# Where the weights begin in their tiles: the halves that stay in the array against those that move

## The chip, the cores and the metric

The kernel runs on one core of one Trainium2 chip. The metric is the time of one execution on the device in microseconds; the median of several runs counts.

## The reference

A decoder trunk of two layers over 256 tokens of width 1,024 in float32. The first layer is differential attention, the second attends with its own queries to a shared K and V (with 256 tokens there is one block of keys, so no others are selected). Each is followed by a squared-ReLU MLP with 4,096 hidden units, and both blocks end in a layer norm.

```python
for layer in range(DEPTH):
    if layer < N_A_LAYERS:
        mix = diff_attention(h, w_in_a[layer], lam_a[layer], subln_a[layer], w_out_a[layer], ...)
    else:
        if kv is None:
            kv = shared_kv(h, w_kv_shared)
        mix = moba_attention(h, w_q_b[j], w_out_b[j], kv[0], kv[1], kv[2], rel_bias)
    h = layer_norm(DEEPNORM_ALPHA * h + mix, ln1_g[layer], ln1_b[layer])
    h = layer_norm(DEEPNORM_ALPHA * h + squared_relu_mlp(h, w_up[layer], w_down[layer]), ...)
```

## The kernel before, in words

All weight matrices are cut into units of 128 x 2,048 numbers, 48 for each layer, in the order in which the program uses them. A unit comes in two pieces of 512 KB into the tiles `raw` (five buffers). ScalarE rounds a piece to a shorter format in `whi` (line 103), VectorE takes the difference, the remainder, to `wlo` (line 115). `whi` and `wlo` have seven buffers each (`AHEAD`), so unit v lies in slot v mod 7, and unit v + 7 waits until v has been used. The activations are split in the same way, into `act_hi` and `act_lo`, in the MLP into `h_hi` and `h_lo`. A product is then three matmuls: high by high, high by low, low by high; `three` issues them. It has two forms:

- *Weights move* (`moving_w`, lines 141 to 143): the activations of 128 tokens are loaded into the array as the stationary operand, and 512 columns of weights stream past. So it is for V, for the attention's output (`mix`), for the first quarter of the MLP's upward product (`up_rows`), and for the downward one (`down`). The end of the last layer's `down` streams 256 columns at a time.
- *Weights stay* (lines 145 to 147): 128 x 128 weights are loaded into the array, and the 256 tokens of `act` stream past. So it is for the queries and keys (`project`, units 2 to 9 in layer 0 and 4 to 11 in layer 1) and for the rest of the upward product (`up`, units 20, 21, 24, 25, and so on to 41 of each layer).

In a call of `nc.tensor.matmul` the output stands first, then the stationary operand, then the moving one; in the profile's rows the moving operand's tile stands first behind the arrow and the stationary one second. While one matmul streams, the weights of the next are loaded (the engine PEld of the profile).

Order: the program is written out by hand, engine by engine. Each `bg` call on the way does some pieces of later units, on ScalarE and VectorE, and starts their transfers on SyncE's queue.

Addresses: pools lie one behind the other in each partition. `act_hi` starts at byte 16,512, `act_lo` at 24,704, the seven `whi` at 70,336 and every 8,192 bytes behind it, the seven `wlo` at 127,680 in the same way. A tile `pad` of 96 bytes (line 64) stands ahead of the pools of the layers, so that `h_hi` and `h_lo` start at 202,368 and 214,656 and every 4,096 behind. Taken within 256 bytes that is 128 for the activations and 192 for the weights. All cuts into these tiles are by multiples of 512 bytes, so each matmul's operand keeps its tile's place within 512 bytes.

Of the kernel before, what the change touches and what calls it, by code (L numbers as in the profile page):

```python
# [21 lines left out]
F32R = mybir.dt.float32r  # L22
# [6 lines left out]
P = 128  # L29
# [13 lines left out]
UNITS = 48  # L43
AHEAD = 7
# [8 lines left out]
def trunk(ctx: ExitStack, tc: tile.TileContext, x, first, units, lam_a, subln, rel_bias,  # L53
# [4 lines left out]
    wpool = ctx.enter_context(tc.tile_pool(name="wpool", bufs=1))  # L58
# [2 lines left out]
    dram = ctx.enter_context(tc.tile_pool(name="dram", bufs=1, space=bass.MemoryType.DRAM))  # L61


    small.tile([P, 24], F32, name="pad", bufs=1)

    def bank(tag):
        return psum.tile([P, 512], F32, name="ps_" + tag, tag=tag,
                         bufs={"a": 4, "b": 2, "c": 2}[tag])

    def split_to(hi, lo, src, scale=None):  # L70

        nc.scalar.activation(hi, src, AF.Copy, scale=1.0 if scale is None else scale)  # L72
        if scale is None:
            nc.vector.tensor_tensor(lo, src, hi.bitcast(F32), op=ALU.subtract)  # L74
        else:
            nc.vector.scalar_tensor_tensor(lo, src, scale, hi.bitcast(F32),
                                           op0=ALU.mult, op1=ALU.subtract)
# [4 lines left out]
    raws, split, used, free = {}, {}, set(), set()  # L82
    state = {"piece": 0, "head": 0, "credit": 0.0}

    def fetch(q):

        if q < NU * PER:
            v, s = divmod(q, PER)
            raws[q] = wpool.tile([P, PIECE], F32, name="raw", bufs=RAWS)
            nc.sync.dma_start(raws[q], units[v, s])  # L90

    def head():

        v, s = divmod(state["head"], PER)
        if v >= NU:
            return False
        if s == 0 and v not in split:
            if v >= AHEAD and v - AHEAD not in free:
                return False
            split[v] = (wpool.tile([P, 2048], F32R, name="whi", bufs=AHEAD),  # L100
                        wpool.tile([P, 2048], F32R, name="wlo", bufs=AHEAD))
        c = slice(s * PIECE, (s + 1) * PIECE)
        nc.scalar.activation(split[v][0][:, c], raws[state["head"]], AF.Copy)  # L103
        state["head"] += 1
        return True

    def piece():

        while state["head"] < state["piece"] + 1 + LEAD and head():
            pass  # L110
        v, s = divmod(state["piece"], PER)
        if state["piece"] == state["head"]:
            return False
        c = slice(s * PIECE, (s + 1) * PIECE)
        nc.vector.tensor_tensor(split[v][1][:, c], raws.pop(state["piece"]), split[v][0][:, c].bitcast(F32),  # L115
                                op=ALU.subtract)
        fetch(state["piece"] + RAWS)
        state["piece"] += 1
        return True
# [35 lines left out]
    def at(k, h):  # L155
        return act[0][:, k, tokens(h)], act[1][:, k, tokens(h)]
# [181 lines left out]
    def attention(layer, u0):  # L338
# [4 lines left out]
        with tc.tile_pool(name=f"attn{layer}", bufs=2) as pool, \  # L343
# [19 lines left out]
            def v_first(u):  # L363

                if u == 0:
                    for h in range(2):
                        pv[0, h] = bank("a")
                split[u] = (wpool.tile([P, 2048], F32R, name="whi", bufs=AHEAD),
                            wpool.tile([P, 2048], F32R, name="wlo", bufs=AHEAD))
                hi, lo = (w.rearrange("p (k c) -> p k c", k=4) for w in split[u])  # L370
                for k in range(4):
                    kk = 4 * u + k
                    split_to(act[0][:, kk], act[1][:, kk], chunks[kk][:, :S])
                    split_to(hi[:, k], lo[:, k], chunks[kk][:, S:])
                    if 2 <= kk < NK - 1:
                        fetch(kk + 2)
                    if kk == 6:
                        nc.scalar.dma_start(scr, line)
                    a = [at(kk, h) for h in range(2)]
                    for h in range(2):  # L380
                        nc.tensor.matmul(pv[0, h], a[h][0], hi[:, k], start=kk == 0, stop=False)  # L381
                    for h in range(2):
                        nc.tensor.matmul(pv[0, h], a[h][1], hi[:, k], start=False, stop=False)
                    for h in range(2):
                        nc.tensor.matmul(pv[0, h], a[h][0], lo[:, k], start=False, stop=kk == NK - 1)
                state["piece"] = state["head"] = (u + 1) * PER
                state["credit"] += PACE
                used.add(u)

            if layer == 0:  # L390
                fetch_chunk(7, V[:, 0, :S + 512])
                v_first(0)
                v_first(1)
                free.update(used)
                bg()
                for h in range(2):
                    v_out(0, h)
            else:
                for h in range(2):
                    for c in range(2):  # L400
                        pv[c, h] = bank("a")
                        for g in range(2):
                            u = u0 + 2 * c + g
                            hi, lo = unit(u, k=4)
                            for k in range(4):
                                three(pv[c, h], (hi[:, k], lo[:, k]), at(4 * g + k, h), True, 1 / 8,
                                      g == 0 and k == 0, g == 1 and k == 3)
                                if (h, c, g) == (0, 1, 1) and k % 2 == 0:
                                    ln_turn(1, k // 2)
                            if h == 1:  # L410
                                used.add(u)
                                bg(2, True)
                        v_out(c, h)
# [567 lines left out]
```

## Time and profile before

| what | value |
|---|---|
| median of 3 runs | 592.87 us (592.8 to 593.11) |
| the profiled execution, its own time | 593.63 us |
| its span | 591.6 us |
| TensorE busy | 580.2 us (98%) |
| weight loads busy | 515.6 us (87%) |
| VectorE busy | 378.5 us (64%) |
| ScalarE busy | 318.3 us (54%) |
| moved by DMA | 113.03 MB, 191 GB/s in the mean |

The span is the time from the first to the last instruction that the profiler saw on the core; around it lie 2.0 us. Busy time of TensorE counts a matmul from its start to its modelled end, and matmuls overlap in the array. So a row's duration says little of how close one follows the other; the starts in the timeline do.

### The profile page before, as it was taken

Reading aid. Unit: us, or ns where it says so; the run is one execution under the profiler, and the core shown is the slowest. Engines: PE = TensorE matmul, PEld = TensorE weight load, DVE = VectorE, ACT = ScalarE, POOL = GpSimd, SP = SyncE. Lnnn points to the kernel's source line nnn. Section 1 sums busy time; section 2 is a strip of 40 time slices with the busy share of each in tenths; the row PEclk is TensorE's granted clock in tenths of the full one; section 3 lists DMA queues with packets and bytes.
Section 4 is the critical chain, followed back from the end, with each engine's and each line's share of the span. In section 5 each row is a group of like instructions: output and inputs, shape, how many; then the busy total and the mean of one; then the engine's idle time right before and its main releaser. Section 6 shows DMA issues by size and latency. Waiting matters only on the chain.

```text
span 591.6 us, 9649 instructions
## 1 busy us (share of the span) xinstructions
PE 580.2 (98%) x3768; PEld 515.6 (87%) x3768; DVE 378.5 (64%) x692; ACT 318.3 (54%) x540; POOL 13.1 (2%) x45
## 2 busy tenths in 40 slices
PE   9999999999999999999999999999999999999993
PEld 7999978889899899898889999878899899899883
DVE  5798778976744644543978677697785544554236
ACT  6676787257654655552447555642785564554100
POOL 2000020000000000000000000000000000000000
PEclk9999999999999999999999999999999999999998
DMA  8996736447745836755259744151798556553002
GB/s 300 327 337 229 243 116 212 174 150 268 271 172 207 277 126 237 248 168 191 83 170 344 256 150 155 54 178 36 242 324 288 175 183 214 187 170 107 1 0 71
DMA packets 35548, 113.03 MB, mean 191 GB/s; under 512 B 3872, under 2 KB 8880, under 8 KB 35504
## 3 DMA queue, kind: packets, MB, share of 16 engines
q1 hardware_dynamic: 34144, 107.95, 53.8%
q0 software_dynamic: 1152, 4.19, 2.4%
q8 instruction: 29, 0.48, 0.3%
q10 hardware_dynamic: 208, 0.29, 0.1%
q14 instruction: 15, 0.12, 0.1%
HBM read 111.35 MB, written 1.07 MB: 190 GB/s over the span
## 4 chain that ended last, share of the span: by engine, by line
PE 97%; DMA 1%; DVE 1%; ACT 0%; SPq 0%; issue 0%; DVEq 0%
PE ps_a L143 13%; PE ps_a L142 13%; PE ps_b L145 13%; PE ps_a L141 13%; PE ps_b L147 12%; PE ps_b L146 12%; PE ps_b L141 4%; PE ps_b L143 4%; PE ps_b L142 4%; PE ps_a L462 2%; PE ps_c L515 1%; PE ps_c L292 1%; DMA raw<-in_first 1%; PE ps_a L550 1%; PE ps_c L776 1%; PE ps_a L381 1%
## 5 line engine op out<-in xcount | busy, mean ns | idle before, releaser
L115 DVE TENSOR_TENSOR wlo<-raw,whi 128x1024 fp32r<-128x1024 f32 x188 | 222.8, 1220 | 55.1 <-ACT whi L103 54.7
L103 ACT ACTIVATE whi<-raw 128x1024 fp32r<-128x1024 f32 x188 | 190.1, 1052 | 71.6 <-PE ps_a L143 52.5
L145 PE MATMUL ps_b<-act_hi,whi 128*128 128x256 f32 x640 | 179.8, 281 | 0.0
L146 PE MATMUL ps_b<-act_lo,whi 128*128 128x256 f32 x640 | 177.5, 277 | 0.0
L147 PE MATMUL ps_b<-act_hi,wlo 128*128 128x256 f32 x640 | 177.5, 277 | 0.0
L145 PEld LDWEIGHTS ps_b<-act_hi,whi 128*128 128x128 f32 x640 | 120.2, 188 | 1.5 <-issue 0.7
L146 PEld LDWEIGHTS ps_b<-act_lo,whi 128*128 128x128 f32 x640 | 120.7, 189 | 0.5
L147 PEld LDWEIGHTS ps_b<-act_hi,wlo 128*128 128x128 f32 x640 | 120.3, 188 | 0.0
L143 PE MATMUL ps_a<-whi,h_lo 128*128 128x512 f32 x248 | 97.7, 394 | 0.0
L142 PE MATMUL ps_a<-wlo,h_hi 128*128 128x512 f32 x248 | 97.2, 392 | 0.0
L141 PE MATMUL ps_a<-whi,h_hi 128*128 128x512 f32 x248 | 96.5, 389 | 0.0
L74 DVE TENSOR_TENSOR h_lo<-sqr,h_hi 128x512 fp32r<-128x512 f32 x24 | 16.6, 693 | 77.7 <-ACT h_hi L72 77.7
L142 PEld LDWEIGHTS ps_a<-wlo,h_hi 128*128 128x128 f32 x248 | 46.6, 188 | 10.3
L141 PEld LDWEIGHTS ps_a<-whi,h_hi 128*128 128x128 f32 x248 | 46.6, 188 | 9.9
L143 PEld LDWEIGHTS ps_a<-whi,h_lo 128*128 128x128 f32 x248 | 46.6, 188 | 9.3
L753 ACT ACTIVATE relu<-ps_b 128x512 f32<-128x512 f32 x32 | 19.1, 596 | 65.9 <-PE ps_b L147 55.0
L482 ACT ACTIVATE t<-t,mx 128x256 f32<-128x256 f32 x64 | 28.4, 445 | 31.5 <-DVE mx L479 31.5
L141 PE MATMUL ps_b<-whi,act_hi 128*128 128x512 f32 x96 | 39.1, 407 | 0.0
L143 PE MATMUL ps_b<-whi,act_lo 128*128 128x512 f32 x96 | 37.7, 393 | 0.0
L142 PE MATMUL ps_b<-wlo,act_hi 128*128 128x512 f32 x96 | 37.6, 391 | 0.0
L141 PE MATMUL ps_a<-whi,act_hi 128*128 128x512 f32 x80 | 32.3, 403 | 0.0
L142 PE MATMUL ps_a<-wlo,act_hi 128*128 128x512 f32 x80 | 31.5, 393 | 0.0
(140 smaller groups left out, 587.3 us busy)
## 6 DMA issues: line engine op xcount, KB each, us to landing
raw<-in_units SPq DMA_DIRECT2D x188, 512.0 KB, 4.6
bias<-scr SPq DMA_DIRECT2D x16, 256.0 KB, 5.3
lnp<-in_ln_g POOLq DMA_DIRECT2D x4, 512.0 KB, 4.5
lnp<-in_ln_b POOLq DMA_DIRECT2D x4, 512.0 KB, 5.4
raw<-in_first SPq DMA_DIRECT2D x5, 384.0 KB, 6.6
xres<-in_x SPq DMA_DIRECT2D x1, 1024.0 KB, 5.9
out<-xres SPq DMA_DIRECT2D x2, 256.0 KB, 2.1
out<-xres SPq DMA_DIRECT2D x4, 128.0 KB, 1.9
```

Source lines behind the costliest of these rows:

```text
L74: nc.vector.tensor_tensor(lo, src, hi.bitcast(F32), op=ALU.subtract)
L103: nc.scalar.activation(split[v][0][:, c], raws[state["head"]], AF.Copy)
L115: nc.vector.tensor_tensor(split[v][1][:, c], raws.pop(state["piece"]), split[v][0][:, c].bitcast(F32), op=ALU.subtract)
L141: nc.tensor.matmul(ps, a[0], w[0], start=start, stop=False)
L142: nc.tensor.matmul(ps, a[0], w[1], start=False, stop=False)
L143: nc.tensor.matmul(ps, a[1], w[0], start=False, stop=stop)
L145: nc.tensor.matmul(ps, w[0], a[0], start=start, stop=False)
L146: nc.tensor.matmul(ps, w[0], a[1], start=False, stop=False)
L147: nc.tensor.matmul(ps, w[1], a[0], start=False, stop=stop)
L462: nc.tensor.matmul(sc[m][:, c:c + n], a[r, q], b[r, :n], start=i == 0, stop=i == 2)
L482: nc.scalar.activation(t[:, m, s], t[:, m, s], AF.Exp, bias=mx[:, m, j:j + 1], accum_out=sm[:, m, j:j + 1])
L753: nc.scalar.activation(r, ps, AF.Relu)
```

## The change

The tiles of `whi` and `wlo` become 128 bytes longer (`SHIFT`, 32 numbers), and a unit's half uses 2,048 of the 2,080 numbers, either from the tile's start or from 128 bytes further. Which of the two depends on the half and on `stationary(v)`, which names the units whose weights stay. Each slot of each half has a tag of its own with one buffer, so that the fourteen tiles lie where they are first asked for: whi and wlo of a slot one behind the other, 8,320 bytes apart.

```diff
+    SHIFT = 32
...
+    def stationary(v):
+
+        layer, n = divmod(v, UNITS)
+        if n < 16:
+            return (2 if layer == 0 else 4) <= n < (10 if layer == 0 else 12)
+        return 20 <= n < 44 and n % 4 < 2
+
+    def new_halves(v):
+        halves = []
+        for i, n in enumerate(("whi", "wlo")):
+            t = wpool.tile([P, 2048 + SHIFT], F32R, name=n, tag=f"{n}{v % AHEAD}", bufs=1)
+            c = SHIFT * ((i + stationary(v)) % 2)
+            halves.append(t[:, c:c + 2048])
+        return tuple(halves)
...
-            split[v] = (wpool.tile([P, 2048], F32R, name="whi", bufs=AHEAD),
-                        wpool.tile([P, 2048], F32R, name="wlo", bufs=AHEAD))
+            split[v] = new_halves(v)
...
-                split[u] = (wpool.tile([P, 2048], F32R, name="whi", bufs=AHEAD),
-                            wpool.tile([P, 2048], F32R, name="wlo", bufs=AHEAD))
+                split[u] = new_halves(u)
```

In the built program the first `whi` starts at 70,336 as before, its `wlo` at 78,656, the next slot's `whi` at 86,976. With the offset in the tile, weights that move start 192 bytes past a multiple of 256, weights that stay 64 past one. `act_hi` and `act_lo` stay where they were. `h_hi` and `h_lo` move 1,792 bytes further, to 204,160 and 216,448, which is still 128 within 256. Within 512 bytes weights that move now start at 192 or at 448, those that stay at 64 or at 320, h at 384 and no longer at 128. The three matmuls, their shapes and operands and the list of instructions on each engine are those of before.

## Rows read from the trace of the kernel before

**Rows 1.** Page, parts 1 and 2: busy time by engine; granted clock in 40 slices.

```profile
PE 580.2 (98%) x3768; PEld 515.6 (87%) x3768; DVE 378.5 (64%) x692; ACT 318.3 (54%) x540; POOL 13.1 (2%) x45
...
PEclk9999999999999999999999999999999999999998
```

**Rows 2.** Page, part 4: the chain that ended last, by engine.

```profile
PE 97%; DMA 1%; DVE 1%; ACT 0%; SPq 0%; issue 0%; DVEq 0%
```

**Rows 3.** Groups by form: 256-wide matmuls; xcount, then busy us, mean ns.

```profile
L145 PE MATMUL ps_b<-act_hi,whi 128*128 128x256 f32 x640 | 179.8, 281 | 0.0
```

**Rows 4.** Groups by form: matmuls of line 141; the last is 256 wide.

```profile
L141 PE MATMUL ps_a<-whi,h_hi 128*128 128x512 f32 x248 | 96.5, 389 | 0.0
...
L141 PE MATMUL ps_b<-whi,act_hi 128*128 128x512 f32 x96 | 39.1, 407 | 0.0
...
L141 PE MATMUL ps_a<-whi,act_hi 128*128 128x512 f32 x80 | 32.3, 403 | 0.0
...
L141 PE MATMUL ps_b<-whi,h_hi 128*128 128x256 f32 x16 | 4.4, 276 | 0.0
```

**Rows 5.** Timeline of TensorE, 162 to 172 us (start us, us, line, operation).

```profile
161.95 0.28 PE L145 MATMUL ps_b<-act_hi,whi 128*128 128x256 f32 x1
...
171.81 0.28 PE L145 MATMUL ps_b<-act_hi,whi 128*128 128x256 f32 x1
```

**Rows 6.** Timeline of TensorE, 139 to 149 us.

```profile
138.85 0.28 PE L145 MATMUL ps_b<-act_hi,whi 128*128 128x256 f32 x1
...
148.74 0.28 PE L145 MATMUL ps_b<-act_hi,whi 128*128 128x256 f32 x1
```

**Rows 7.** Timeline of TensorE, 216 to 226 us.

```profile
215.94 0.39 PE L141 MATMUL ps_a<-whi,h_hi 128*128 128x512 f32 x1
...
226.24 0.39 PE L141 MATMUL ps_a<-whi,h_hi 128*128 128x512 f32 x1
```

**Rows 8.** Timeline of TensorE, 100 to 111 us.

```profile
100.08 0.40 PE L141 MATMUL ps_b<-whi,act_hi 128*128 128x512 f32 x1
...
110.58 0.40 PE L141 MATMUL ps_a<-whi,act_hi 128*128 128x512 f32 x1
```

**Rows 9.** Stretches: us, PE busy (xmatmuls), granted clock, DMA share, GB/s.

```profile
28.85:33.85 5.00, 5.00 (x45) 1.00 1.03 404
50.55:52.75 2.20, 2.20 (x21) 1.00 0.82 272
65.65:67.85 2.20, 2.20 (x21) 1.00 0.99 385
138.85:149.45 10.60, 10.60 (x92) 1.00 0.75 250
316.45:327.45 11.00, 11.00 (x95) 1.00 0.96 353
428.65:439.25 10.60, 10.60 (x93) 1.00 0.91 292
17.30:27.00 9.70, 9.70 (x88) 1.00 0.97 343
```

**Rows 10.** Timeline of TensorE, line 145, 183 to 188 us.

```profile
183.14 0.28 PE L145 MATMUL ps_b<-act_hi,whi 128*128 128x256 f32 x1
...
183.84 0.28 PE L145 MATMUL ps_b<-act_hi,whi 128*128 128x256 f32 x1
...
187.93 0.28 PE L145 MATMUL ps_b<-act_hi,whi 128*128 128x256 f32 x1
```

**Rows 11.** Timeline of TensorE, 577 to 581.5 us.

```profile
576.99 0.28 PE L141 MATMUL ps_b<-whi,h_hi 128*128 128x256 f32 x1
...
581.41 0.28 PE L141 MATMUL ps_b<-whi,h_hi 128*128 128x256 f32 x1
```

**Rows 12.** Groups by form: the pieces of the weights' halves.

```profile
L115 DVE TENSOR_TENSOR wlo<-raw,whi 128x1024 fp32r<-128x1024 f32 x188 | 222.8, 1220 | 55.1 <-ACT whi L103 54.7
...
L103 ACT ACTIVATE whi<-raw 128x1024 fp32r<-128x1024 f32 x188 | 190.1, 1052 | 71.6 <-PE ps_a L143 52.5 <-DMA raw<-in_units 17.4 <-DVE wlo L115 1.5
```

## Prediction

> **What bounds the kernel now.** I read the page from the top. TensorE is busy for 580.2 of 591.6 us, 98%, and the clock it is granted is 9 tenths or more in all slices but the last, which is the higher of its two levels, 2.4 GHz [rows 1]. VectorE is at 64% and ScalarE at 54%. The chain of work that ended last runs over TensorE for 97% [rows 2]. So work that becomes shorter elsewhere buys nothing, and the time is the number of matmuls times the distance from one matmul's start to the next one's. This distance, which I call the beat, is what a change of addresses can touch. The "mean ns" of a matmul in the groups is not the beat: it holds the pipeline's depth (281 ns for a matmul that is followed by the next after some 113).
>
> Two kinds make up nearly all of the work. In the first the weights stay in the array and 256 columns of activations stream past: 640 matmuls on each of three lines, 1,920 in all (one of the three stands in [rows 3]). In the second the activations stay and 512 columns of weights stream: 248, 96 and 80 on each of three lines, 1,272 [rows 4]. The reader is to take the beat from the timeline, by dividing the distance between two rows of the same line by the triples between them.
>
> Done that way, the first kind has **two beats**. From 161.95 to 171.81 us there are 29 triples of 340 ns, 113.3 ns a matmul, the short beat [rows 5]. From 138.85 to 148.74 us, the same lines and shapes, there are 28 triples of 353 ns, 117.7 ns a matmul, the long beat [rows 6]. The second kind has two as well: 15 triples of 687 ns, 228.9 a matmul, from 215.94 us [rows 7], and 15 of 700 ns, 233.3 a matmul, from 100.08 us [rows 8]. In both kinds the long beat is 4.4 ns longer.
>
> Where is the long beat? A set of them begins where the stream was broken (by transposes, scores or a wait) and lasts to the next break. In the first kind I find six long sets, in the six first stretches of [rows 9]: 42, 18, 18, 90, 93 and 90 matmuls, together 351 (a stretch's own count also holds the two or three that were begun before it, or end it). There are also ten units that follow a block of the second kind without a break; they begin with two long triples and then change to the short beat, as at 183.14 us [rows 10]. That is 60 more, 411 of 1,920, or 21%. In the second kind the one long set is that of [rows 8], 48 of 1,272, or 4%. The transfers do not sort them: a stretch at the long beat has a DMA share of 1.03, but another 0.75, and the one in the last row, at the short beat, 0.97 [rows 9].
>
> **What the change does to this, part by part.**
>
> 1. *The addresses.* In the kernel before, every start in the weights' tiles is 192 bytes past a multiple of 256, and every start in act and in h is 128 past one. While a matmul streams, the next one's stationary operand is read. The start of that operand less the start of the moving one is therefore 128 - 192 = -64, or 192 within 256, for the second kind, and 192 - 128 = 64 for the first. The change puts weights that stay at 64 within 256 and leaves the others at 192, so the first kind's difference becomes 64 - 128 = -64 as well. The second kind keeps its own within 256 bytes.
>
> 2. *What a difference of 192 is worth at 256 columns.* The trace has one such place: the last 48 matmuls of the second layer's products are of the second kind, but 256 wide (16 on each line, the last of [rows 4]). From 576.99 to 581.41 us they go at 13 triples of 340 ns, 113.3 a matmul, exactly the short beat, and from the first triple on, right behind 512-wide ones [rows 11]. So the short beat is the same with either difference, and a stretch that has it now gains nothing: 0 for 1,509 matmuls. What differs is the entry: two long triples with 64, none with 192. And with 192 long beats are rarer, 4% against 21%. Both point one way, and both are thin: one place, and one set.
>
> 3. *The gain.* The lower bound is 0: the long beat could depend on the break alone. The upper bound is all long beats of the first kind, 411 x 4.4 ns = 1.8 us. I take the share that the second kind shows under the difference that the first will have: (21% - 4%) x 1,920 x 4.4 ns = **1.4 us**, since [rows 8] says that this difference does not exclude the long beat.
>
> 4. *Names by slot, and 128 bytes more in each tile.* The list of instructions on each engine, and what each waits for, is the same; unit v lies in slot v mod 7, where the rotation over seven buffers had put it. Cost 0. The pieces that ScalarE and VectorE write begin elsewhere, 188 of each at 1,052 and 1,220 ns [rows 12]; I cost that at 0 too. If one of them took 1% more, it would be 2 us over the whole run on engines that idle for over a third of it; the cover goes only where a unit is due just as its last piece is written.
>
> 5. *What the longer tiles also do.* Two tiles that follow each other now lie 8,320 bytes apart, not 8,192. Within 256 bytes that is corrected, but within 512 it is not: weights that move start at 192 in one tile and at 448 in another, h moves from 128 to 384 and act stays. If only 256 bytes count, this is nothing. The trace before cannot show the contrary, because all its starts agree within 512. I bound it by the two beats of the second kind: about half of 1,272 matmuls see another difference, 636 x 4.4 ns = 2.8 us slower if they fall to the long beat. Below, a triple takes 687 ns where two of half its width take 680; that is 2.2 ns a matmul, and 636 x 2.2 ns = 1.4 us would be the gain if that went. I take 0, since the 512-wide beat is alike over all seven slots and both column halves, whose starts differ by 512 and by 8,192.
>
> The sum is -1.4 us on a profiled execution of 593.63 us (span 591.6 and 2.0 around it). That execution is 0.8 us above the median of the runs, 592.87; the difference carries over: 592.87 - 1.4 = **591.4 us**, 0.24% faster. A measurement of this kernel can tell about 0.2%, or 1.2 us, from no change, so the forecast lies just past that bound.
>
> **The rivals.**
>
> *No change.* The long beat is a matter of where a break leaves the loads and the streams against each other, and the difference of addresses has no part in it. For it: the short beat is the same with 64 and with 192 [rows 5, 11], 48 long beats in a row exist with 192 [rows 8], and long beats fall on many slots. Against it: the entry of [rows 10] beside that of [rows 11]. Then the long beats stay or are dealt anew, within some 0.5 us: 592.9. The Trainium skill says this more strongly. In "TensorE: Matmul & The Clock Gate", section "Step-by-step: what each phase is for", the moving operand and the weight load have read ports of their own, and a load takes no bandwidth from the running matmul; by that rule no address matters and the time is 592.9. That the short beat is the same at both differences agrees with it; two beats of one instruction it does not explain.
>
> *Slower, by the upper half of 512.* As in part 5: the starts of moving weights alternate between 192 and 448 from tile to tile, and the 512-wide matmuls of about half of the tiles fall to 233.3. This decides from 2.6 us up, which would outweigh the gain by the bound above; 592.87 + 2.8 = 595.7 us without the gain. For it: the change has the alternation, and the beat is an affair of operands that are read together. Against it: nothing in the trace has yet depended on a start.
>
> *Slower, by a long beat that stays.* With the new difference a first-kind stretch that falls into the long beat at entry does not leave it, as at 100 us. If all 1,509 short beats went that way, it would be 6.6 us: 599.5. Against it stands [rows 11], where the short beat holds.
>
> **How the numbers follow.** The forecast gets 0.42, no change 0.33, the upper half of 512 0.17 and the staying long beat 0.08. So faster 0.42, same 0.33, slower 0.25. The low end takes the whole of the first kind's long beats (1.8 us), 0.2 us for the set of [rows 8] and part of the 1.4 us of part 5: 590.2. The high end is the first slower rival, 595.7. What is left out is the last rival and the tail of the others.
>
> **What would show it.** Right: in the profile of the changed kernel the first-kind stretches at the places of [rows 6, 9] go at 340 ns a triple, units behind a 512-wide block have no long triples at entry, and the 512-wide beat stays at 687 ns a triple in every slot. The whole gain is then between 1 and 2 us. No change: sets of 353 ns stay, at these or other breaks. Wrong: 512-wide triples of 700 ns in every other tile (the first slower rival), or 353 ns throughout the units after the feed-forward's first ones (the second). A beat that neither trace has had, at 256 or at 512, would make the whole argument wrong, since it takes all its prices from the two beats. So would an idle TensorE before a unit's first matmul with ScalarE or VectorE as what ended it.

## The result and the profile after

The changed kernel takes 599.75 us (599.38 to 600.0), the kernel before 592.99 us in the runs of the same comparison: a ratio of 1.0107 on record, 95% interval 1.0095 to 1.012 (the two medians by themselves give 1.0114). It became slower by 6.8 us where 1.4 us less was forecast. The profiled execution took 599.74 us, its span is 597.6 us, 6.0 more than before.

First the page: busy time by engine, the granted clock, and the chain that ended last by engine.

```profile
PE 585.6 (98%) x3768; PEld 520.6 (87%) x3768; DVE 378.1 (63%) x692; ACT 318.8 (53%) x540; POOL 12.9 (2%) x45
...
PEclk9999999999999999999999999999999999999997
...
PE 97%; DMA 1%; DVE 1%; ACT 0%; SPq 0%; issue 0%; DVEq 0%
```

TensorE has 3,768 matmuls as before and 98% of the span, and the chain runs over it for 97%, as in [rows 1, 2]; the clock it is granted is the same in all slices but the last. No engine and no wait has taken a part of the chain. The matmuls themselves follow each other more slowly. The groups by form show it faintly (xcount, then busy us and mean ns):

```profile
L161 PE MATMUL ps_b<-act_hi,whi 128*128 128x256 f32 x640 | 181.0, 283 | 0.0
...
L157 PE MATMUL ps_a<-whi,h_hi 128*128 128x512 f32 x248 | 97.9, 395 | 0.0
```

Line 161 (145 before) has gone from 281 to 283 ns [rows 3], for this column holds the depth of the pipeline and not the beat. The timeline shows the beat. At the place of [rows 5], in the same unit of the same layer:

```profile
162.35 0.28 PE L161 MATMUL ps_b<-act_hi,whi 128*128 128x256 f32 x1
...
172.95 0.28 PE L161 MATMUL ps_b<-act_hi,whi 128*128 128x256 f32 x1
```

30 triples in 10.60 us, 353 ns each, where [rows 5] had 340. Like the unit of [rows 10] it comes in at the long beat, but it does not leave it. So it is in all ten units behind a 512-wide block: 32 long triples each, where the kernel before had two and then 30 short ones. At the place of [rows 6] nothing has changed: 29 triples of 353 ns.

```profile
139.61 0.28 PE L161 MATMUL ps_b<-act_hi,whi 128*128 128x256 f32 x1
...
149.86 0.28 PE L161 MATMUL ps_b<-act_hi,whi 128*128 128x256 f32 x1
```

The 512-wide beat is still 687 ns, as in [rows 7]: 13 triples in 8.93 us.

```profile
218.60 0.39 PE L157 MATMUL ps_a<-whi,h_hi 128*128 128x512 f32 x1
...
227.53 0.39 PE L157 MATMUL ps_a<-whi,h_hi 128*128 128x512 f32 x1
```

Counted over the whole trace, 565 of the 655 triples of 256 columns are now at the long beat, before they were 142; 38 are left at the short one, before 456 (the others hold a break or a change of beat). 423 triples more at 13.3 ns are 5.6 us, and 300 of them lie in those ten units. Summed another way, over the starts of the 1,882 matmuls with weights that stay and no break behind them, these took 215.5 us before and 221.0 now, the last 256-wide ones 0.2 more, the opening (up to the first unit, which waits for its inputs) 0.4 more and the 512-wide ones 0.1 less: 6.0 us in all.

Two things do not fit "192 means long". The 38 short triples lie in five stretches behind breaks, and every stretch of weights that stay now has the difference 192. One of them is at 29.64 us, 12 triples in 4.08 us, just where the kernel before had a long set:

```profile
29.64 0.28 PE L161 MATMUL ps_b<-act_hi,whi 128*128 128x256 f32 x1
...
33.72 0.28 PE L161 MATMUL ps_b<-act_hi,whi 128*128 128x256 f32 x1
```

And the last 256-wide products, whose difference is 192 in both kernels, went at 340 ns in [rows 11] and go at 353 or 354 now, 13 triples in 4.60 us:

```profile
582.78 0.28 PE L157 MATMUL ps_b<-whi,h_hi 128*128 128x256 f32 x1
...
587.38 0.28 PE L157 MATMUL ps_b<-whi,h_hi 128*128 128x256 f32 x1
```

So the difference alone does not fix the beat. The experiments had to say what does.

### The profile page after: what moved, and what is told of

It reads as the page before. It is cut to its first block, busy times and chain, and to the rows that moved or that the text cites. A ratio compares the mean times of both kernels' runs of the same rounds, so it can differ in the third digit from the quotient of the medians.

```text
span 597.6 us, 9649 instructions
## 1 busy us (share of the span) xinstructions
PE 585.6 (98%) x3768; PEld 520.6 (87%) x3768; DVE 378.1 (63%) x692; ACT 318.8 (53%) x540; POOL 12.9 (2%) x45
## 4 chain that ended last, share of the span: by engine, by line
PE 97%; DMA 1%; DVE 1%; ACT 0%; SPq 0%; issue 0%; DVEq 0%
PE ps_b L161 13%; PE ps_a L157 13%; PE ps_a L159 13%; PE ps_b L163 13%; PE ps_b L162 13%; PE ps_a L158 12%; PE ps_b L157 4%; PE ps_b L159 4%; PE ps_b L158 4%; PE ps_a L477 2%; PE ps_c L530 1%; PE ps_c L308 1%; DMA raw<-in_first 1%; PE ps_a L565 1%; PE ps_c L791 1%; PE ps_a L396 1%
## 5 line engine op out<-in xcount | busy, mean ns | idle before, releaser
L157 PE MATMUL ps_a<-whi,h_hi 128*128 128x512 f32 x248 | 97.9, 395 | 0.0
```

What stands on the lines that cost most here:

```text
L157: nc.tensor.matmul(ps, a[0], w[0], start=start, stop=False)
```

## The experiments

The theories behind the expectations: A, the difference of the stationary and the moving start within 256 bytes decides; A', the place of the moving start counts too; B, starts that alternate within 512 bytes; C, which tile lies behind which; D, any move deals the beats anew by chance. The comparisons are with the kernel before on the same chip.

### One part at a time

The first run keeps the names by slot and drops the shift:

```diff
-    SHIFT = 32
+    SHIFT = 0
```

> The change with SHIFT = 0: names by slot and whi and wlo of a slot one behind the other, but no longer tiles and no shift; all starts are again 192 within 256 and alike within 512. Theory A (the difference of stationary and moving start within 256 bytes decides): 593 us, 256-wide triples at 340 ns as before. Theory B (starts that alternate within 512 bytes decide): 593 us. Theory C (which tile lies behind which): 599.7 us with 353 ns. Theory D (any move of addresses or of time deals the entries anew): anything between 591 and 600 us, long beats at other places.

Measured: 593.75 us, ratio 1.0003 (0.9993 to 1.0012). The new order of the tiles costs nothing; C is out. (Only the times of this run are used.)

The second keeps the longer tiles and their alternation within 512 bytes, and leaves every start at 192 within 256:

```diff
-            c = SHIFT * ((i + stationary(v)) % 2)
+            c = SHIFT * (i % 2)
```

> The change with tiles 128 bytes longer, but every unit's weights, staying or moving, at 192 within 256 as before; within 512 the tiles alternate between 192 and 448, as in the change. Theory A (difference within 256): the difference of the 256-wide matmuls is 64 again, so 593 us and 340 ns a triple. Theory B (alternation within 512): 599.7 us and 353 ns. Theory C: 599.7 us if the order of tiles did it, 593 us if not. Theory D: 591 to 600 us.

Measured: 593.39 us, ratio 0.9999 (0.999 to 1.0008). In its timeline the unit of [rows 5] goes at 340 ns, 30 triples in 10.22 us (the first of them, the unit's second, is still long, as at the entry in [rows 10]); 142 long triples in all, exactly as many as before.

```profile
160.77 0.28 PE L161 MATMUL ps_b<-act_hi,whi 128*128 128x256 f32 x1
...
170.99 0.28 PE L161 MATMUL ps_b<-act_hi,whi 128*128 128x256 f32 x1
```

This run differs from the change in one thing, where the weights that stay begin. B is out, and with it the price that was kept for the upper half of 512; the 6 us belong to those 128 bytes.

The third moves all weights to 64 within 256:

```diff
-            c = SHIFT * ((i + stationary(v)) % 2)
+            c = SHIFT * ((i + 1) % 2)
```

> The change with every unit's weights at 64 within 256, the moving ones too; within 512 they alternate. Theory A: the 256-wide matmuls have the change's difference of 192, so 353 ns a triple as in the change; the 512-wide ones get a difference of 64, which they never had, and keep 687 ns if they don't care: 599.7 us, more or less by up to 5.6 us if they do. Theory B: 599.7 us, since the alternation is the same. Theory D: 591 to 600 us.

Measured: 603.88 us, ratio 1.0175 (1.0158 to 1.0192). The 256-wide triples are long in 492 cases. The 512-wide ones, whose difference became 64, are at 700 ns for most of the run (11 triples in 7.70 us here), which adds 5.0 us over the starts:

```profile
222.12 0.39 PE L157 MATMUL ps_a<-whi,h_hi 128*128 128x512 f32 x1
...
229.82 0.40 PE L157 MATMUL ps_a<-whi,h_hi 128*128 128x512 f32 x1
```

So the same 64 that allows the short beat at 256 columns is bad at 512. The two forms want different differences.

### The beats by difference, measured by themselves

Three kernels hold nothing but sets of matmuls on copies of one piece of a unit. Once the first block is through, no other engine works while a set runs, so no other engine's work makes these beats.

```diff
+        for r in range(2):
+            for d in (0, 16, 32, 48, 64, 80, 96, 112):
+                if r == 0:
+                    entry()
+                else:
+                    nc.scalar.activation(o[:, :512], pb, AF.Copy)
+                stay(0, 0, d, d)
```

`stay` is 32 triples of the first kind with the weights' start d numbers past the moving one's, `entry` a block of 512-wide ones with difference 192. A number has 4 bytes, so d = 16 is 64 bytes. In the two kernels after this one a set has 16 triples.

> Leaves out the whole computation of the reference: sets of 96 matmuls of 256 columns, weights staying, on copies of one piece of a unit, with the weights' start 0, 64, 128 ... 448 bytes past the moving operand's within 512; each set comes once behind 48 matmuls of 512 columns and once behind a wait for ScalarE; then six sets with high and low halves at unlike starts, and ten sets of 96 matmuls of 512 columns. Theory A: the sets at 192 (and 448, if 256 counts) go at 353 ns a triple, those at 64 and 320 at 340 ns behind a 512-wide block. Theory B: sets whose halves agree within 512 go at 340 ns, those with the halves at 64 and 320 at 353 ns. Theory D: no order by start, some sets at 340 and some at 353 ns for the same start in the two passes.

The timeline of this run, each time the first and the last row of one line in a set of 32 triples. The first four sets are 256 wide with the differences 0, 64, 128 and 192, the fifth is 512 wide with the difference 0:

```profile
32.21 0.28 PE L94 MATMUL ps_b<-act_hi,whi 128*128 128x256 f32 x1
...
43.36 0.28 PE L94 MATMUL ps_b<-act_hi,whi 128*128 128x256 f32 x1
...
54.92 0.28 PE L94 MATMUL ps_b<-act_hi,whi 128*128 128x256 f32 x1
...
65.48 0.28 PE L94 MATMUL ps_b<-act_hi,whi 128*128 128x256 f32 x1
...
76.81 0.28 PE L94 MATMUL ps_b<-act_hi,whi 128*128 128x256 f32 x1
...
87.85 0.28 PE L94 MATMUL ps_b<-act_hi,whi 128*128 128x256 f32 x1
...
99.21 0.28 PE L94 MATMUL ps_b<-act_hi,whi 128*128 128x256 f32 x1
...
110.16 0.28 PE L94 MATMUL ps_b<-act_hi,whi 128*128 128x256 f32 x1
...
442.63 0.39 PE L104 MATMUL ps_a<-whi,h_hi 128*128 128x512 f32 x1
...
463.72 0.39 PE L104 MATMUL ps_a<-whi,h_hi 128*128 128x512 f32 x1
```

Divided by the 31 triples between the rows: 360, 341 (340 from the second triple on), 356, 353 and 680 ns. The differences 256 to 448 repeat 0 to 192, and the second pass, behind a wait, repeats the first. The 512-wide sets of this run went at 680 (difference 0), 700 (64), 697 (128, in the mean) and 687 ns (192). High and low halves at 64 and 320 went at 340 like halves at 64 and 64: within 512 bytes only what is left within 256 counts. A is borne out as far as the size goes, B and D fall again. One thing disturbed A: two sets with difference 64, but with the moving start at 384 and at 0 within 512, stayed at 353.

The next run asks whether the place counts:

```diff
+                for a in range(0, 128, 16):
+                    if r == 0:
+                        entry()
+                    else:
+                        nc.scalar.activation(o[:, :512], pb, AF.Copy)
+                    stay(a, a, a + d, a + d)
```

> Leaves out the whole computation of the reference: sets of 48 matmuls of 256 columns with the difference 64, then 192, and the moving start at each of eight places 64 bytes apart within 512; the same with 64 behind a wait for ScalarE; then sets of 48 matmuls of 512 columns with the differences 0 and 192 at four places. Theory A: one beat for each difference wherever the moving start is: 340 at 64, 353 at 192, and 680 and 687 at 512 columns. Theory A': at 64 the beat is 340 at some places and 353 at others, the same places behind a 512-wide block and behind a wait. Theory D: no order by place.

Difference 192 went at 353 in all eight places. Difference 64 went at 340 in six of eight places behind a 512-wide block, and in all eight behind a wait. The same start, 384 within 512 with difference 64, in both ways (first and last row of each set):

```profile
48.75 0.28 PE L92 MATMUL ps_b<-act_hi,whi 128*128 128x256 f32 x1
...
53.70 0.28 PE L92 MATMUL ps_b<-act_hi,whi 128*128 128x256 f32 x1
...
213.06 0.28 PE L92 MATMUL ps_b<-act_hi,whi 128*128 128x256 f32 x1
...
217.48 0.28 PE L92 MATMUL ps_b<-act_hi,whi 128*128 128x256 f32 x1
```

14 triples of 353 or 354 ns, then 13 of 340. So the place alone does not decide: **at one and the same difference two beats can hold, and what stood before the set picks one.** Behind 512-wide sets of difference 0, difference 64 went to 353 in all four cases; behind three more of difference 192 it did so twice, and one set that followed another of difference 64 without a break changed from 340 to 353. The 512-wide sets went at 680 in all four places with difference 0; with 192 two went at 687 and two at 700.

The last of the three tests the way in directly: pairs of a 512-wide and a 256-wide set on the same tiles, and narrow matmuls put between two sets. `wide(16, 16, 16, 16)` is a 512-wide set with difference 0; the narrow matmuls have difference 64, like the set behind them.

```diff
+        for n in (32, 64, 128, 192):
+            for m in (1, 2):
+                wide(16, 16, 16, 16)
+                for _ in range(m):
+                    nc.tensor.matmul(pa[:, :n], cut(wt[0], 16, 128), cut(act[0], 0, n), start=True, stop=True)
+                stay(0, 0, 16, 16)
```

> Leaves out the whole computation of the reference. First five pairs of sets, 48 matmuls of 512 columns with moving weights and 48 of 256 columns on the same tiles and starts, difference 192, as at the end of the last layer, with h at 128 or 384 and the weights' halves at 192 or 448 within 512. If 192 has one beat, all five 256-wide sets go at 353 ns; if it has two and the way in decides, as in the kernel before, the one with 128 and 192 goes at 340 ns and others may; if places within 512 count, exactly those with unlike halves go at 353. Then 15 pairs: 48 matmuls of 512 columns with difference 0, then 48 of 256 columns, weights staying, with the halves' differences from 0 to 192 in seven ways, and with difference 64 behind one or two matmuls of 32, 64, 128 or 192 columns. If the phase of the way in picks the beat, some of these narrow matmuls end the 353 ns that difference 64 had behind difference 0 and give 340; if the history of differences picks it, none does.

Its timeline, first and last row of four sets: weights moving at the very starts of [rows 11]; difference 64 behind difference 0; halves at 64 and 192 behind difference 0; difference 64 behind difference 0 with one matmul of 64 columns between:

```profile
31.58 0.28 PE L103 MATMUL ps_a<-whi,h_hi 128*128 128x256 f32 x1
...
36.53 0.28 PE L103 MATMUL ps_a<-whi,h_hi 128*128 128x256 f32 x1
...
114.42 0.28 PE L92 MATMUL ps_b<-act_hi,whi 128*128 128x256 f32 x1
...
119.72 0.28 PE L92 MATMUL ps_b<-act_hi,whi 128*128 128x256 f32 x1
...
198.03 0.28 PE L92 MATMUL ps_b<-act_hi,whi 128*128 128x256 f32 x1
...
202.45 0.28 PE L92 MATMUL ps_b<-act_hi,whi 128*128 128x256 f32 x1
...
264.22 0.28 PE L92 MATMUL ps_b<-act_hi,whi 128*128 128x256 f32 x1
...
268.99 0.28 PE L92 MATMUL ps_b<-act_hi,whi 128*128 128x256 f32 x1
```

353 or 354 (14 triples in 4.95 us), 353, 340, and 341 (14 triples in 4.77 us, the first of them longer). A single narrow matmul turns the long beat into the short one. One of 64 or 192 columns does, one of 32 or 128 does not; two of 64 or of 128 do, two of 32 or 192 do not. The differences that went before are the same in all eight cases, so their history alone does not pick. How loads and streams stand to each other in time at the entry, their phase, would fit, but no run shows it. Each of these cases ran once. That chance does not pick rests on more: at difference 64 all ten sets behind a wait went at 340 in these kernels, all five directly behind difference 0 at 353, and the second run above has the very number of long triples of the kernel before. Halves with *unlike* differences, 64 for the high and 192 for the low, went to the short beat from the third triple on, where 64 and 64 could not; the other five mixtures took 353 to 360.

All five pairs at difference 192 gave 353, the starts of [rows 11] among them. But the place of [rows 11] itself is no single case. Six of the whole kernels have difference 192 there, and four go at 340: the kernel before, the second run above, the kernel moved by 128 bytes and the one with unlike halves (both below). The changed kernel and the one with difference 0 for weights that stay go at 353. The row pair is that of the second run, 14 triples in 4.76 us:

```profile
576.16 0.28 PE L157 MATMUL ps_b<-whi,h_hi 128*128 128x256 f32 x1
...
580.92 0.28 PE L157 MATMUL ps_b<-whi,h_hi 128*128 128x256 f32 x1
```

So 192 has two beats at 256 columns as well. Which way in gives its short one was not found.

### What follows in the kernel

Moving everything by 128 bytes changes no difference:

```diff
+    const.tile([P, 32], F32, name="front")
     act = (const.tile([P, NK, S], F32R, name="act_hi"),
```

> The kernel before with 128 bytes more at the front, so that every tile behind it moves by 128 and no difference changes. Theory A alone (only differences count): 593 us, long sets as before. Theory A' (the moving start itself counts too: in the map, difference 64 went to 340 ns with the moving start at 256 within 512, and stayed at 353 ns at 384 and 0): act now starts at 256 within 512, so the six long sets go to 340 ns and 591.2 us is read.

Measured: 593.51 us, ratio 1.0001 (0.9992 to 1.001), with 156 long triples. A' is out; a place by itself is worth nothing.

Next the difference of weights that move, from 192 to 0, since the map has 680 there against 687:

```diff
-    SHIFT = 32
+    SLACK = 48
...
+            begins = 192 + 192 * (2 * (v % AHEAD) + i)
+            c = ((192 if stationary(v) else 128) - begins) % 256 // 4
```

> Weights that move start at 128 within 256, as act and h do (difference 0), weights that stay at 192 (difference 64, as before); tiles 192 bytes longer, the pad 128 bytes longer, one buffer in place of two for the discarded squares. Theory A, with the map's beats: the 1,272 matmuls of 512 columns go from 687 to 680 ns a triple, 2.2 ns each, 2.8 us; the 256-wide ones stay at 340 with their long sets: 590.2 us. Theory A': the 512-wide beat depends on the place of the moving start too, and the map's 680 at 256 and 0 within 512 does not hold at 128: 593 us. Theory D: 591 to 600 us.

Measured: 596.0 us, ratio 1.0044 (1.0031 to 1.0057): a miss. The 512-wide matmuls without a break behind them in either kernel gave 2.3 us back: 325 of 424 triples are at 680, and 44 more, nearly all of them the first of a block, at 687 or 700. But the units behind them, with their difference of 64 untouched, come in another way and are now long, 417 triples against 142. At the place of [rows 5]:

```profile
161.18 0.28 PE L162 MATMUL ps_b<-act_hi,whi 128*128 128x256 f32 x1
...
172.13 0.28 PE L162 MATMUL ps_b<-act_hi,whi 128*128 128x256 f32 x1
```

31 triples in 10.95 us, 353 ns each. That is 3.7 us over the starts, and 1.4 us more lay in two breaks (below). It is the clearest single sign that the way in picks: these matmuls' own starts are as far apart within 256 bytes as before.

The opposite, weights that stay at difference 0 (the edit is against the run before):

```diff
-            c = ((192 if stationary(v) else 128) - begins) % 256 // 4
+            c = ((128 if stationary(v) else 192) - begins) % 256 // 4
```

> The tiles of the run with difference 0 for weights that move, but the other way round: weights that move at 192 within 256 as before (difference 192, 687 ns a triple), weights that stay at 128, like act (difference 0). Theory A, with the map's 360 ns: about 655 triples of 256 columns, of which 513 are at 340 and 142 at 353 ns before, all go to 360: 513 x 20 + 142 x 7 ns = 11.3 us more than before, 604.5 us. Theory D: 591 to 600 us.

Measured: 607.39 us, ratio 1.0236 (1.0218 to 1.0253). The triples do go at 360 ns, as in this stretch, 28 triples in 10.07 us. Over the starts that is 10.1 us in all, where 11.3 were expected:

```profile
141.21 0.28 PE L162 MATMUL ps_b<-act_hi,whi 128*128 128x256 f32 x1
...
151.28 0.28 PE L162 MATMUL ps_b<-act_hi,whi 128*128 128x256 f32 x1
```

Not in the expectation were 2.2 us from 512-wide triples at 700 ns, which now come in behind another beat (187 of them, before 21), and 1.1 from the two breaks.

Then halves with unlike differences, which the third of the small kernels had found. Half of the change is undone: of weights that stay only the low half begins at 64 (the edit is against the change).

```diff
-            c = SHIFT * ((i + stationary(v)) % 2)
+            c = SHIFT * (i % 2 and not stationary(v))
```

> The change with half of it undone: of weights that stay only the low halves begin at 64 within 256 (difference 192), the high ones at 192 as before (difference 64); weights that move at 192. The map had this pair of differences at 340 ns a triple even behind difference 0, where 64 and 64 stayed at 353. Theory A (each load's own difference decides, two of three loads here are of high halves): if the pair has the short beat only, the 142 triples at 353 ns before go to 340 and the kernel takes 593.4 - 1.9 = 591.5 us; if the way in still picks, 592 to 594 us. If a shifted half costs by its share, a third of the change's 6.4 us: 595.5 us.

Measured: 592.76 us, ratio 0.9985 (0.9976 to 0.9994). 20 long triples are left. The place of [rows 6], long in both other kernels, is short: 29 triples in 9.86 us.

```profile
138.94 0.28 PE L161 MATMUL ps_b<-act_hi,whi 128*128 128x256 f32 x1
...
148.80 0.28 PE L161 MATMUL ps_b<-act_hi,whi 128*128 128x256 f32 x1
```

The gain is 0.9 us and not 1.9: over the starts it is 0.9 as well, because the triples that have neither beat or hold a break have gone from 57 to 104. 34 of them take 357 to 363 ns, at the starts of sets.

With difference 0 for weights that move in addition (`c` from 128 for those, 192 and 64 for the halves that stay):

> As the run before it, but weights that move start at 128 within 256, like act and h (difference 0, 680 ns a triple of 512 columns in the map against 687). Theory A: 2.8 us less than the run before it, 588.7 us, if the pair of differences 64 and 192 keeps the 256-wide triples at 340 ns. If the way in picks the long beat there as it did with 64 and 64 behind difference 0: 596 us.

Measured: 591.71 us, ratio 0.9964 (0.9952 to 0.9977), 3.0 above the expectation. Against the kernel before, 512-wide matmuls take 2.2 us less, those with weights that stay 1.2 less, the last 256-wide ones, now at difference 0, 0.3 more. Two breaks are 1.3 us longer; the two other runs with difference 0 have the same two. One is an output product that waits for VectorE:

```profile
99.70 0.40 PE L159 MATMUL ps_b<-wlo,act_hi 128*128 128x512 f32 x1
...
100.79 0.51 PE L160 MATMUL ps_b<-whi,act_lo 128*128 128x512 f32 x1 [0.69 <-DVE act_lo L78]
```

The matmul of line 160 starts 1.09 us after the one before it, where this distance was 0.24. The three kernels with difference 0 had one buffer for the discarded squares, to make room for longer tiles; the last run gives the second back (the edit is against the run before):

```diff
-                        sq = small.tile([P, P], F32, name="sq", bufs=1)
+                        sq = small.tile([P, P], F32, name="sq")
...
-        lp = small.tile([P, 2, 64], F32, name="lp", bufs=1)
+        lp = early[:, 1792:1920].rearrange("p (a b) -> p a b", a=2)
```

> As the run with difference 0 for weights that move and 64 and 192 for the halves that stay, but the discarded squares have their two buffers again; the room comes from the product for lambda, which goes to a free part of the tile of its inputs. In that run two breaks ahead of the first layer's output product lasted 1.3 us longer than before. If the one buffer made them (a square that waits for the one before it), they go and the kernel takes 591.7 - 1.3 = 590.4 us; if the shifted starts made them, 591.7 us.

Measured: 590.9 us, ratio 0.9952 (0.9938 to 0.9966). The two breaks are back at their length of before, with the shifted starts as they were, so the one buffer had made them. This version is 0.5% faster than the kernel before and beats both kernels. Its timeline has the short beat at the place of [rows 6] and 680 ns at 512 columns (26 triples in 8.84 us, 11 in 7.48):

```profile
139.89 0.28 PE L162 MATMUL ps_b<-act_hi,whi 128*128 128x256 f32 x1
...
148.73 0.28 PE L162 MATMUL ps_b<-act_hi,whi 128*128 128x256 f32 x1
...
151.93 0.39 PE L158 MATMUL ps_a<-whi,h_hi 128*128 128x512 f32 x1
...
159.41 0.39 PE L158 MATMUL ps_a<-whi,h_hi 128*128 128x512 f32 x1
```

## Why the prediction was wrong, point by point

- *What bounds the kernel: right.* TensorE has 97% of the chain in both traces, and only its beats changed.
- *Two beats and their prices: right.* 340 and 353, 687 and 700 ns come back in the later runs at the same differences, and 423 triples at 13.3 ns are 5.6 of the 6.0 us. (The 142 long triples of the kernel before are 426 matmuls; the prediction counted 411.)
- *Part 1, the addresses: right.* The difference within 256 bytes went from 64 to 192 for weights that stay, and the run that left this out alone takes 593.39 us.
- *Part 2, the price of 0 for the 1,509 matmuls at the short beat: the step that failed.* That the short beat is 340 ns with either difference is true. What did not follow is that a stretch that has it keeps it, and that with 192 a unit behind a 512-wide block comes in without long triples. This rested on the one place of [rows 11]. In the changed kernel those ten units come in long and stay long, and 565 triples of 655 are at 353; the price should have been up to 4.4 ns a matmul. The small kernels put 19 sets of 256 columns wholly at difference 192, behind wide blocks and behind waits, and all went at 353, while difference 64 went at 340 in 25 of 41 sets. That [rows 11] went at 340 was its way in, as far as the runs go: the same products go at 353 in the changed kernel, at the same difference.
- *Part 3, the share of long beats: wrong in sign for that reason.* It carried the 4% of the second kind over to the first; the triples of 256 columns have 86% under that difference (565 of 655). 512 and 256 columns want different differences: 64 allows 340 ns at 256 and makes 700 at 512, 0 is best at 512 and makes 360 at 256.
- *Part 4, names by slot and longer tiles at 0: right*, by the first two experiments.
- *Part 5, the upper half of 512: right to take 0*; its bound of 2.8 us, which set the high end, was never paid.
- *The rivals.* "No change" falls, since the second experiment and the change differ in nothing but the 128 bytes; its thought that the entry decides between two beats was half of the truth. The Trainium skill ("TensorE: Matmul & The Clock Gate", "Step-by-step: what each phase is for") gives the load and the stream read ports of their own and lets a load take no read bandwidth from the running matmul. By that rule alone no start would matter; here the start of the load's operand against the stream's makes 340 to 360 ns of the same three matmuls, and the measurement decides. What in the memory or the ports makes the difference, no run shows. "A long beat that stays" is what happened, with the sign that the prediction named for it: 353 ns throughout the units. It had 0.08 and lay outside the range; its mechanism had been seen at 512 columns, at 100 us [rows 8], and was given the small chance because of [rows 11]. That its 599.5 us meet 599.75 is in part luck: it counts all 1,509 matmuls, 6.6 us, where 423 triples, 1,269 matmuls, changed beat for 5.6 us, and 0.4 more came from the opening.

## What to carry to other kernels

Where TensorE has the chain, read the beat from starts in the timeline, not from mean durations, and test where operands begin: here 64 bytes of placement were worth up to 6% of a matmul's beat. Measure the differences in a small kernel of nothing but matmuls before the layout is changed, for each width by itself, and again behind the kind of block that precedes them in the kernel. One place in a trace is not a rule, however clean its rows.

## What was not expected of the hardware

Of the stationary start less the moving one, only what is left within 256 bytes counted. The beats of a triple whose loads all have one difference, in ns (for 128 in the mean, since its triples differ):

| difference | 256 columns | 512 columns |
|---|---|---|
| 0 | 360 | 680 |
| 64 | 340, or 353 after some ways in | 700 |
| 128 | 356 | 697 |
| 192 | 353, or 340 after some ways in | 687, or 700 after some ways in |

Behind the first one to three triples the beat held to the end of nearly every set, and one matmul of 64 columns ahead of a set could change it. So a better beat in one stage can make the next stage's worse, as with 2.3 us won at 512 columns and 3.7 lost at 256 behind them. Differences other than multiples of 64 bytes were not tried.
